# Second-norm vectors spread by TensorE instead of a broadcast load, and a rearranged routing, in a two-layer retention, convolution and MoE step

## Chip, cores and metric

The kernel runs on one core of one Trainium2 chip. The metric is the device time of one execution in microseconds (us). All matrices are float32; where it matters a matrix product is made from a high and a low part in the fp32r format. Engines are named as in the profile: PE is TensorE, DVE VectorE, ACT ScalarE, POOL GpSimd, and SP the queue that issues most DMAs.

## What is computed

256 tokens (128 of a prompt, 128 of a sample, `NT` = 2 tiles) of width 1024 go through two layers. Each layer is a token mixer, a norm, a mixture of experts and a second norm:

```python
for i in range(DEPTH):                     # DEPTH = 2
    sh1, sc1, g1, sh2, sc2, g2 = split(silu(cond) @ ada_w[i] + ada_b[i], 6)
    h = x * (1 + sc1) + sh1
    y = retention(h) if i == 0 else short_conv(h)
    x = layer_norm(ALPHA * x + g1 * y, ln_g[i, 0], ln_b[i, 0])
    h = x * (1 + sc2) + sh2
    y = moe_ffn(h)                         # 64 experts, top 6 of 4 of 8 groups, plus one shared
    x = layer_norm(ALPHA * x + g2 * y, ln_g[i, 1], ln_b[i, 1])
```

In `moe_ffn` the score of a group is the sum of its two best experts, the four best groups are kept, and of the experts in them the six best.

## The kernel before

**Weights.** All weights, some 500 MB, pass once through a ring of 14 slots of 1 MB in SBUF (`Stream`). The loads are written into SP's queue in the order of the program: a unit is issued when the unit 14 places before it has been marked as used. Every other load that SP issues stands in the same queue, in order: `spread` (L537) is such a load, one row of DRAM written to all 128 partitions, 512 KB for a vector of 1024.

**Order.** Within a stage each engine works through its instructions in the order of the program; waits between engines are semaphores. Tiles are taken by tag: a new tile of a tag waits until the readers of the last one of that tag are done. The PSUM banks 0 to 3 are such tags too (`bank`; `rtbank` alternates between banks 2 and 3).

**Stages.** Retention with its adaLN matmuls; the first norm and the router (`ln1`, `router`, `router_turn`); the choice of experts (`route`); 24 blocks of experts (`moe`); the second norm, which also makes the modulated input of the next mixer (`ln2_next`); the convolution (`conv`); then norm, router, choice and blocks of layer 1, and `ln2_out`. Between the last blocks of a layer stands a branch (`overflow`) that all engines reach.

**First norm and routing.** `ln1` makes the input of the MoE, `hf`, for the two tiles. `parts` splits it: ScalarE rounds it to H (L1034), GpSimd subtracts to get the low part L (L1035). `router_turn` makes scores and the best groups (`gr`, in which the entries of the four kept groups are replaced by HIT). `route` turns that into a mask: L1142 to L1147 make a group mask and a penalty and apply them, L1150 takes the maxima, L1154 to L1156 give `maskb`, TensorE counts (L1160 to L1166, into two banks `bk` and `cnt`), L1171 and L1277 (in `slots`) make the 0/1 matrix P0 of slots, and L1176 to L1192 the weights and the order of the experts; L1185 and L1187 read `cnt`. `moe` then gathers the tokens of the first four blocks by matmuls with P0 (`gather`, L1305; four calls on banks 0, 1, 2, 3, each with 8 matmuls on H and L, copied out by L1309), and the first expert matmul (L1343) follows.

**Second norm of layer 0.** The normalised value stands in tile `g2`, tag G. TensorE turns it, and `mod_evac` makes the convolution's input as H and L (L670 to L677). `ln2_gb` has issued two broadcast loads of ln_g and ln_b to tiles of tags T5 and T6; GpSimd multiplies both by ALPHA (L1532) and updates x by

```python
nc.gpsimd.tensor_mul(self.x[:, t], xh, lgb[0])              # L1002, xh is a half of tile G
nc.gpsimd.tensor_add(self.x[:, t], self.x[:, t], lgb[1])    # L1003
```

for each of the two tiles.

**Convolution.** `conv` takes a new tile of tag G and writes the product of two projections to it (L1610, L1613), after which L1618 and L1620 convolve it. Its weights come in pieces of 512 columns: ScalarE rounds a piece to its high half (L139), VectorE subtracts to get the low half (L140), both inputs in SBUF, and TensorE uses a piece in 12 matmuls (L691 to L693). Four pieces make a projection (`proj_T`), four pieces fit in SBUF at a time, and adaLN matmuls (L503) stand between the projections.

**End of layer 1.** `end` issues the two broadcasts of ln_g and ln_b to tag H after the branch and ahead of the last two blocks; `ln2_out` uses them.

Of the kernel before, what the change touches and what calls it, by code (L numbers as in the profile page):

```python
# [7 lines left out]
F32 = mybir.dt.float32  # L8
# [3 lines left out]
AF = mybir.ActivationFunctionType  # L12
OP = mybir.AluOpType
AX = mybir.AxisListType

D = 1024
KD = 8
NT = 2
# [5 lines left out]
ALPHA = (2.0 * 2) ** 0.25  # L24
EPS = 1e-5
SENT = 3.0e38
HIT = 3.2e38
HIT_T = 3.1e38
# [43 lines left out]
class Kernel:  # L72
# [343 lines left out]
    def load_layer_consts(self, l):  # L416
        I, q = self.I, self.nc.sync
        q.dma_start(out=self.rb, in_=I["moe_bias"][l:l + 1].to_broadcast([128, NEXP]))
        for t in range(NT):
            for j, n in ((0, "ln_g"), (64, "ln_b")):  # L420
                q.dma_start(out=self.lnr[j + t:j + 64:32], in_=I[n][l, 0].rearrange("(h c) -> h c", h=2))

    def load_router(self, l):
        self.rw = self.w([128, KD, NEXP], F32, "S3")
# [580 lines left out]
    def ln1(self, ada=False):  # L1005


        nc = self.nc
        hf = []
        g = self.g1  # L1010
        self.ln_open(g, hf)
        mu, rs, _ = self.ln_x
        self.h2T = [self.w([128, 4, NT * 128], F32, f"T{7 + i}") for i in range(2)]

        def scale(t):
            nc.vector.scalar_tensor_tensor(self.A[t], g[:, t], mu[t], self.A[t], op0=OP.add, op1=OP.mult)

        def norm(t):
            v = [x.rearrange("n (p j) -> n p j", j=KD) for x in (self.A[t], self.B[t])]
            for h in range(2):  # L1020
                js = slice(4 * h, 4 * h + 4)
                nc.vector.scalar_tensor_tensor(hf[t].rearrange("n (j p) -> n p j", j=KD)[:, :, js], v[0][:, :, js], rs[t],
                                               v[1][:, :, js], op0=OP.mult, op1=OP.add)

        def turn(t):
            for half in range(2):
                bk = self.pjbank()
                for c in range(4):
                    k = 4 * half + c
                    nc.tensor.transpose(bk[:, 128 * c:128 * (c + 1)], hf[t][:, 128 * k:128 * (k + 1)], self.ident)  # L1030
                nc.scalar.copy(self.h2T[half][:, :, 128 * t:128 * (t + 1)], bk.rearrange("p (c n) -> p c n", c=4))

        def parts(t):
            nc.scalar.copy(H[:, t], hf[t])  # L1034
            nc.gpsimd.tensor_sub(L[:, t], hf[t], H[:, t].bitcast(F32))  # L1035

        hf.append(self.w([128, D], F32, "W", 4))
        for h in range(2):
            self.ln_part(0, h)
        scale(0)  # L1040
        self.table(AF.Sigmoid)
        self.ln_part(1, 0)
        norm(0)
        turn(0)
        hf.append(self.w([128, D], F32, "W", 4))
        self.ln_part(1, 1)
        self.router(0)
        scale(1)
        norm(1)
        self.h2 = [self.w([128, NT, D], F32R, "H"), self.w([128, NT, D], F32R, "L")]  # L1050
        H, L = self.h2
        if ada:
            bk = self.ada_mm(1, 0, range(4, 6), self.free_acc(0), True, False)
        self.warm(self.WN[ada])
        turn(1)
        self.router_turn(0)
        self.router(1)
        self.router_turn(1)
        parts(0)
        parts(1)  # L1060
        self.table(AF.Silu)
        if ada:
            self.ada_mm(1, 0, range(6, 8), bk)
            self.ada_bk = bk
        self.warm(self.WN[2 + ada])
# [68 lines left out]
    def route(self, l):  # L1134
        nc = self.nc
        V = nc.vector
        sc = self.scores
        tmp, gr = self.rtmp, self.gr
        sel = mask = tmp[:, 0:128].rearrange("p (t e) -> p t e", t=NT)
        gmask = self.w([128, NT, 8], F32, "gmask")  # L1140
        pen = self.w([128, NT, 8], F32, "pen")
        V.tensor_scalar(gmask, gr[:, :, 0:8], HIT_T, None, op0=OP.is_ge)  # L1142
        V.tensor_scalar(pen, gmask, 1.0, SENT, op0=OP.subtract, op1=OP.mult)
        sm = self.selm[:, :, 0:64].rearrange("p t (g e) -> p t g e", e=8)
        V.tensor_mul(sm, sel.rearrange("p t (g e) -> p t g e", e=8),
                     gmask[:, :, :, None].to_broadcast([128, NT, 8, 8]))
        V.tensor_add(sm, sm, pen[:, :, :, None].to_broadcast([128, NT, 8, 8]))  # L1147
        m8 = self.w([128, NT, 8], F32, "m8")
        for t in range(NT):
            V.max(out=m8[:, t], in_=self.selm[:, t, 0:64])  # L1150
        V.memset(m8[:, :, 6:8], SENT)
        res = tmp[:, 260:392].rearrange("p (t e) -> p t e", t=NT)
# [5 lines left out]
        bk = self.rtbank()  # L1158
# [6 lines left out]
        for t in range(NT):  # L1165
# [5 lines left out]
        V.scalar_tensor_tensor(self.r1, bk[:, 0:128].rearrange("p (t e) -> p t e", t=2), 1.0, mask,  # L1171
                               op0=OP.add, op1=OP.mult)
        self.P0 = self.slots(0, self.r1)
        ws = self.w([128, NT], F32, "ws")
        for t in range(NT):
            V.scalar_tensor_tensor(self.comb[:, t], sc[:, t], 1.0, mask[:, t], op0=OP.mult, op1=OP.mult,  # L1176
# [116 lines left out]
    def gather(self, P, xg, q, j2, b=2):  # L1293
# [14 lines left out]
                    n += 1  # L1308
        nc.scalar.copy(xg[j2 // 2][:, 2 * (j2 % 2):2 * (j2 % 2) + 2], bk.rearrange("p (c n) -> p c n", c=2))  # L1309

    def slot_T(self, Pc, i):

        nc = self.nc
        o = 128 * (i % 4)
        bk = self.bank(2)
        for t in range(NT):
            nc.tensor.transpose(bk[:, 128 * t:128 * (t + 1)], Pc[:, t, o:o + 128], self.ident)
        PT = self.w([128, NT * 128], F32R, f"S{i % 2}")
        cb = self.w([128, 1], F32, "cb", 2)
        nc.vector.tensor_scalar(PT, bk[:, 0:256], 0.0, None, op0=OP.is_gt)  # L1320
        nc.vector.tensor_reduce(out=cb, in_=bk[:, 0:256], axis=AX.X, op=OP.add)
        return PT, cb

    def moe(self, l, fill, first):
        self.new_acc()
        for n, i in enumerate((self.SH[0],) * 2 + (self.SH[1],) * 2 + (self.SH[2],)):
            fill.setdefault(i, []).append((self.shared, l, n))
        nc, U, st = self.nc, self.U, self.st
        n = self.nb
        P, C, X, G = {}, {}, {}, {}  # L1330
# [57 lines left out]
        nq = n // 2  # L1388
        prep(0)
        C[0] = self.weighted(P[0], 0)  # L1390
        for j in range(4):
            self.gather(P[0], X[0], 0, j, j)
        for f in first:
            f()
        fill.setdefault(0, []).insert(0, (self.order,))
# [54 lines left out]
            pair(i)  # L1450

        def end():
            if l == self.layers - 1:
                t = self.w([128, 2, D], F32, "H")
                self.ln2_gb(l, [t[:, 0], t[:, 1]])
            self.ln_open(self.g2, [self.w([128, D], F32, f"T{7 + t}") for t in range(NT)])
            for i in range(n - self.END, n):
                pair(i)
# [46 lines left out]
        for t in range(NT):  # L1505
            self.spread(self.g2[:, t], self.vecs[1][t, 1:2])

    def ln2_gb(self, l, tiles):

        self.lgb = tiles  # L1510
        for x, n in zip(tiles, ("ln_g", "ln_b")):
            self.spread(x, self.I[n][l, 1:2])

    def ln2_next(self):

        nc = self.nc
        g = self.g2
        mu, rs, nm = self.ln_x
        self.ln2_gb(0, [self.w([128, D], F32, "T5"), self.w([128, D], F32, "T6")])
        banks = [[self.bank(2 * t + h) for h in range(2)] for t in range(NT)]  # L1520
        for t in range(NT):
            nc.vector.tensor_scalar(g[:, t], g[:, t], mu[t], rs[t], op0=OP.add, op1=OP.mult)
        ks = range(self.HEAD1)
        ada = self.ada_mm(1, 1, ks, self.free_acc(0), True)
        for t in range(NT):
            for h in range(2):
                self.mod_T(t, g[:, t], h, banks[t][h])
        self.warm(self.WN[4], self.free_acc(1))
        self.mod_evac(banks, self.a1, self.b1)
        self.ada_sum(1, 1, ks, ada)  # L1530
        for i in range(2):
            nc.gpsimd.tensor_scalar(self.lgb[i], self.lgb[i], ALPHA, 1.0, op0=OP.mult, op1=OP.mult)  # L1532
        for t in range(NT):
            self.next_x(t, g[:, t], self.lgb)

# [193 lines left out]
```

## Time and profile before

| what | value |
|---|---|
| median of 3 runs | 1470.44 us (1468.39 to 1474.17) |
| the profiled execution | 1470.57 us |
| its span, first to last instruction | 1468.8 us |
| TensorE busy | 1305.3 us, 89% of the span |
| VectorE, ScalarE, GpSimd busy | 475.8, 396.7, 101.6 us |
| moved by DMA | 535.32 MB, mean 364 GB/s |
| mean granted clock of TensorE | 0.959 |

The span is what the trace covers; the execution's own time is a little longer. A granted clock of 1.0 is 2.4 GHz, 0.5 is 1.2 GHz. Busy time of TensorE holds matmuls that are pipelined, so a busy TensorE is not one at its peak. A DMA share of 1 means that all 16 DMA engines were busy.

### The profile page before, as it was taken

Reading aid. Unit: us, or ns where it says so; the run is one execution under the profiler, and the core shown is the slowest. Engines: PE = TensorE matmul, PEld = TensorE weight load, DVE = VectorE, ACT = ScalarE, POOL = GpSimd, SP = SyncE. Lnnn points to the kernel's source line nnn. Section 1 sums busy time; section 2 is a strip of 40 time slices with the busy share of each in tenths; the row PEclk is TensorE's granted clock in tenths of the full one; section 3 lists DMA queues with packets and bytes.
Section 4 is the critical chain, followed back from the end, with each engine's and each line's share of the span. In section 5 each row is a group of like instructions: output and inputs, shape, how many; then the busy total and the mean of one; then the engine's idle time right before and its main releaser. Section 6 shows DMA issues by size and latency. Waiting matters only on the chain. (4 is left out here: it accounts for less than half of the span.)

```text
span 1468.8 us, 21018 instructions
## 1 busy us (share of the span) xinstructions
PE 1305.3 (89%) x7542; PEld 711.2 (48%) x7542; DVE 475.8 (32%) x943; ACT 396.7 (27%) x704; POOL 101.6 (7%) x140
## 2 busy tenths in 40 slices
PE   6899999889999889998768699799999889998774
PEld 4788888544435323443214488654445224443211
DVE  4665656732121111211004366822211011121004
ACT  5654545422221012221103234422221012221001
POOL 3120110230000000000001300220000000000001
PEclk9999999999999989999988899999999999999998
DMA  9999796989999999999999998679999999999995
GB/s 286 324 382 349 261 333 244 349 318 375 408 391 415 413 407 413 412 398 409 411 368 393 364 386 301 229 242 394 398 398 411 411 403 413 408 393 409 397 364 197
DMA packets 169343, 535.32 MB, mean 364 GB/s; under 512 B 14212, under 2 KB 65596, under 8 KB 148244
## 3 DMA queue, kind: packets, MB, share of 16 engines
q1 hardware_dynamic: 166148, 529.25, 94.3%
q10 hardware_dynamic: 2768, 4.60, 0.9%
q8 instruction: 62, 1.02, 0.3%
q14 instruction: 45, 0.37, 0.1%
q0 software_dynamic: 320, 0.08, 0.0%
HBM read 528.57 MB, written 5.31 MB: 363 GB/s over the span
## 5 line engine op out<-in xcount | busy, mean ns | idle before, releaser
L1343 PE MATMUL b<-ring,W 128*32 128x512 f32 (+1 forms) x2048 | 440.9, 626 | 63.6 <-DMA ring<-in_moe_w_up 59.2
L1374 DVE SCALAR_TENSOR_TENSOR Y<-b,cb,Y 128x512 fp32r<-128x512 f32 x92 | 69.1, 751 | 675.0 <-ACT Y L1373 675.0
L1343 PEld LDWEIGHTS b<-ring,W 128*32 128x32 f32 (+1 forms) x2048 | 104.4, 124 | 293.4 <-issue 268.1
L1370 PE MATMUL b<-ring,mtmp 128*32 128x512 f32 (+1 forms) x1024 | 221.8, 631 | 17.6 <-DMA ring<-in_moe_w_down 17.3
L1373 ACT ACTIVATE Y<-b,cb 128x512 fp32r<-128x512 f32 x92 | 63.2, 687 | 423.7 <-PE b L1370 393.4
L140 DVE TENSOR_TENSOR W<-ring,W 128x512 fp32r<-128x512 f32 x198 | 135.5, 707 | 91.8 <-ACT W L139 91.4
L139 ACT CAST W<-ring 128x512 fp32r<-128x512 f32 x197 | 117.9, 621 | 105.7 <-PE b L693 78.2
L1370 PEld LDWEIGHTS b<-ring,mtmp 128*32 128x32 f32 (+1 forms) x1024 | 58.4, 130 | 160.6 <-issue 101.9
L691 PE MATMUL b<-H,W 128*128 128x256 f32 x400 | 115.6, 289 | 14.3 <-DVE G L1613 12.1
L693 PE MATMUL b<-H,W 128*128 128x256 f32 x400 | 114.3, 286 | 4.2 <-DVE W L140 4.2
L692 PE MATMUL b<-L,W 128*128 128x256 f32 x400 | 114.1, 285 | 0.1
L1305 PE MATMUL b<-T,H 128*128 128x256 f32 x384 | 99.9, 293 | 6.5 <-ACT W L1309 1.5
L121 PE MATMUL acc<-Y,S 128*128 128x512 f32 x368 | 100.6, 396 | 0.0
L1305 PEld LDWEIGHTS b<-T,H 128*128 128x128 f32 x384 | 72.8, 190 | 52.7 <-PE b L1343 41.0
L1305 PE MATMUL b<-T,L 128*128 128x256 f32 x384 | 95.5, 283 | 0.0
L691 PEld LDWEIGHTS b<-H,W 128*128 128x128 f32 x400 | 77.7, 194 | 24.1 <-issue 13.8
L1309 ACT COPY W<-b 128x512 f32<-128x512 f32 x96 | 56.4, 587 | 105.6 <-PE b L1305 105.6
L693 PEld LDWEIGHTS b<-H,W 128*128 128x128 f32 x400 | 77.6, 194 | 4.7 <-DVE W L140 4.5
L692 PEld LDWEIGHTS b<-L,W 128*128 128x128 f32 x400 | 77.6, 194 | 0.4 <-issue 0.3
L1305 PEld LDWEIGHTS b<-T,L 128*128 128x128 f32 x384 | 73.2, 191 | 0.0
L121 PEld LDWEIGHTS acc<-Y,S 128*128 128x128 f32 x368 | 63.0, 188 | 11.8 <-issue 3.4
L995 POOL TENSOR_SCALAR lnst<-lnst 128x1 f32<-128x1 f32 x8 | 1.8, 230 | 880.9 <-DVE G L988 485.9
(327 smaller groups left out, 1283.8 us busy)
## 6 DMA issues: line engine op xcount, KB each, us to landing
ring<-in_moe_w_gate SPq DMA_DIRECT2D x256, 512.0 KB
ring<-in_moe_w_up SPq DMA_DIRECT2D x256, 512.0 KB
ring<-in_moe_w_down SPq DMA_DIRECT2D x120, 1024.0 KB
ring<-in_ada_w SPq DMA_DIRECT2D x48, 1024.0 KB
ring<-in_ret_w_in SPq DMA_DIRECT2D x20, 1024.0 KB
ring<-in_conv_w_in SPq DMA_DIRECT2D x12, 1024.0 KB
ring<-in_ret_w_out SPq DMA_DIRECT2D x8, 1024.0 KB
ring<-in_moe_w_down SPq DMA_DIRECT2D x16, 512.0 KB
```

What stands on the lines that cost most here:

```text
L121: self.nc.tensor.matmul(self.acc[t][h], lhsT, rhs, start=s, stop=stop, skip_group_check=True)
L139: (copy or nc.scalar.copy)(hi, src)
L140: nc.vector.tensor_sub(lo, src, hi.bitcast(F32))
L691: nc.tensor.matmul(o, hi[:, c], H[:, k], start=(k == 0), stop=False)
L692: nc.tensor.matmul(o, hi[:, c], L[:, k], start=False, stop=False)
L693: nc.tensor.matmul(o, lo[:, c], H[:, k], start=False, stop=(k == KD - 1))
L1305: nc.tensor.matmul(o, part[:, t, 128 * j:128 * (j + 1)], P[:, t, s0:s0 + 256], start=(n == 0), stop=(n == 3))
L1309: nc.scalar.copy(xg[j2 // 2][:, 2 * (j2 % 2):2 * (j2 % 2) + 2], bk.rearrange("p (c n) -> p c n", c=2))
L1343: nc.tensor.matmul(G[0][m * e:m * (e + 1)], xg[k // 4][:, k % 4, o + m * e:o + m * (e + 1)], w[:, :, k % 4], start=(k == 0), stop=(k == KD ...
L1370: nc.tensor.matmul(bk[m * e:m * (e + 1)], hT[:, k, m * e:m * (e + 1)], w[:, k, 512 * h:512 * (h + 1)], start=(k == 0), stop=(k == 1))
L1373: nc.scalar.activation(hi, bk, AF.Copy, scale=cb)
L1374: nc.vector.scalar_tensor_tensor(lo, bk, cb, hi.bitcast(F32), op0=OP.mult, op1=OP.subtract)
```

## The change

- `load_layer_consts` loads a third row beside the two that it loads twice: ln_g and ln_b of the second norm go to partitions 2, 34, 66 and 98 of the tile `lnr` (two small loads more per layer).
- `ln2_gb` no longer loads. After block 11 of each layer TensorE multiplies a column of the identity, repeated 128 times, with `lnr`, which puts one half of ln_g or ln_b on all partitions; ScalarE copies it to a tile of tag G1 and multiplies by ALPHA on the way in layer 0. The four broadcast loads (two in `ln2_next`, two in `end`) and GpSimd's two multiplications L1532 are gone.
- The low parts L of the MoE input are made by VectorE, in `route` behind P0 and ahead of the weights and the order of the experts.
- The four instructions of the group mask are replaced by one per tile, the minimum of `gr` - HIT_T and the score.
- The first gather goes over H of both tiles, then L of both tiles, and writes all four banks in each of these four rounds; the copies follow at the end.

```diff
     def load_layer_consts(self, l):
-        for t in range(NT):
+        for i, t in ((0, 0), (0, 1), (1, 2)):
             for j, n in ((0, "ln_g"), (64, "ln_b")):
-                q.dma_start(out=self.lnr[j + t:j + 64:32], in_=I[n][l, 0].rearrange("(h c) -> h c", h=2))
+                q.dma_start(out=self.lnr[j + t:j + 64:32], in_=I[n][l, i].rearrange("(h c) -> h c", h=2))
...
-        def parts(t):
-            nc.scalar.copy(H[:, t], hf[t])
-            nc.gpsimd.tensor_sub(L[:, t], hf[t], H[:, t].bitcast(F32))
...
-        parts(0)
-        parts(1)
+        for t in range(NT):
+            nc.scalar.copy(H[:, t], hf[t])
+        self.hf = hf
...
-        gmask = self.w([128, NT, 8], F32, "gmask")
-        pen = self.w([128, NT, 8], F32, "pen")
-        V.tensor_scalar(gmask, gr[:, :, 0:8], HIT_T, None, op0=OP.is_ge)
-        V.tensor_scalar(pen, gmask, 1.0, SENT, op0=OP.subtract, op1=OP.mult)
-        sm = self.selm[:, :, 0:64].rearrange("p t (g e) -> p t g e", e=8)
-        V.tensor_mul(sm, sel.rearrange("p t (g e) -> p t g e", e=8),
-                     gmask[:, :, :, None].to_broadcast([128, NT, 8, 8]))
-        V.tensor_add(sm, sm, pen[:, :, :, None].to_broadcast([128, NT, 8, 8]))
         m8 = self.w([128, NT, 8], F32, "m8")
         for t in range(NT):
+
+            V.scalar_tensor_tensor(self.selm[:, t, 0:64].rearrange("p (g e) -> p g e", e=8),
+                                   gr[:, t, 0:8, None].to_broadcast([128, 8, 8]), HIT_T,
+                                   sel[:, t].rearrange("p (g e) -> p g e", e=8), op0=OP.subtract, op1=OP.min)
             V.max(out=m8[:, t], in_=self.selm[:, t, 0:64])
...
         self.P0 = self.slots(0, self.r1)
+        for t in range(NT):
+            H, L = self.h2
+            V.tensor_sub(L[:, t], self.hf[t], H[:, t].bitcast(F32))
         ws = self.w([128, NT], F32, "ws")
...
+    def gather_first(self, P, xg):
+
+        nc = self.nc
+        bks = [self.bank(j) for j in range(4)]
+        for n, (t, part) in enumerate((t, p) for p in self.h2 for t in range(NT)):
+            for j in range(KD):
+                nc.tensor.matmul(bks[j // 2][:, 256 * (j % 2):256 * (j % 2 + 1)], part[:, t, 128 * j:128 * (j + 1)],
+                                 P[:, t, 0:256], start=(n == j % 2 == 0), stop=(n == 3), skip_group_check=True)
+        for j, bk in enumerate(bks):
+            nc.scalar.copy(xg[j // 2][:, 2 * (j % 2):2 * (j % 2) + 2], bk.rearrange("p (c n) -> p c n", c=2))
...
+        fill.setdefault(self.SH[2] + 1, []).append((self.ln2_gb, ALPHA if l + 1 < self.layers else 1.0))
...
-        for j in range(4):
-            self.gather(P[0], X[0], 0, j, j)
+        self.gather_first(P[0], X[0])
...
-            if l == self.layers - 1:
-                t = self.w([128, 2, D], F32, "H")
-                self.ln2_gb(l, [t[:, 0], t[:, 1]])
...
-    def ln2_gb(self, l, tiles):
-
-        self.lgb = tiles
-        for x, n in zip(tiles, ("ln_g", "ln_b")):
-            self.spread(x, self.I[n][l, 1:2])
+    def ln2_gb(self, scale):
+
+        g = self.w([128, 2, D], F32, "G1")
+        self.lgb = [g[:, 0], g[:, 1]]
+        for j in range(4):
+            bk = self.bank(2 + j % 2)
+            r = 32 * j + 2
+            self.nc.tensor.matmul(bk, self.ident[:, r:r + 1].to_broadcast([128, 128]), self.lnr, start=True, stop=True)
+            self.nc.scalar.activation(g[:, j // 2, 512 * (j % 2):512 * (j % 2 + 1)], bk, AF.Copy, scale=scale)
...
-        self.ln2_gb(0, [self.w([128, D], F32, "T5"), self.w([128, D], F32, "T6")])
...
-        for i in range(2):
-            nc.gpsimd.tensor_scalar(self.lgb[i], self.lgb[i], ALPHA, 1.0, op0=OP.mult, op1=OP.mult)
```

## Rows read from the trace of the kernel before

**Rows 1.** Page: busy tenths of the DMA engines in 40 slices.
```profile
DMA  9999796989999999999999998679999999999995
```

**Rows 2.** Windows: busy us (instructions) of each engine, granted clock, DMA share, GB/s.
```profile
core 0: us, PE busy (x) PEld busy (x) DVE busy (x) ACT busy (x) POOL busy (x), PEclk, DMA share, GB/s
829.20:841.20 12.00, 0.00 (x1) 0.03 (x1) 0.82 (x3) 0.00 (x0) 9.99 (x6) 0.67 1.02 369
...
846.60:850.20 3.60, 3.60 (x18) 3.60 (x18) 2.91 (x8) 0.87 (x2) 0.00 (x0) 0.50 0.99 396
821.60:825.20 3.60, 3.60 (x32) 3.60 (x31) 0.73 (x2) 1.24 (x2) 0.00 (x0) 1.00 1.05 392
```

**Rows 3.** TensorE's waits, 840 to 940 us: total us, times, longest us.
```profile
PE b L691 <- DVE G L1613: 12.1, 1, 12.1
PE b L693 <- DVE W L140: 4.2, 1, 4.2
```

**Rows 4.** Timeline, second norm of layer 0: start, us, instruction, [idle before <- releaser].
```profile
803.80 2.52 POOL L677 TENSOR_TENSOR L<-T,H 128x1024 fp32r<-128x1024 f32 x1 [3.32 <-ACT H L676]
...
804.70 2.71 DVE L677 TENSOR_TENSOR L<-T,H 128x1024 fp32r<-128x1024 f32 x1 [0.60 <-ACT H L676]
...
807.08 1.22 POOL L489 DMA_DIRECT2D adaS<-in_ada_b  x2 [0.29 <-POOL adaS L486]
...
820.28 1.07 PE L503 MATMUL b<-ring,cs 128*32 128x512 f32 x8
...
825.04 0.33 SPq L537 DMA_DIRECT2D T<-in_ln_g  x1
...
829.66 1.04 POOL L1532 TENSOR_SCALAR T<-T 128x1024 f32<-128x1024 f32 x1 [21.36 <-DMA T<-in_ln_g]
...
840.23 0.43 DVE L1610 TENSOR_TENSOR G<-b,mtmp 128x256 f32<-128x256 f32 x1 [17.89 <-POOL x L1002]
```

**Rows 5.** Timeline, routing of layer 0.
```profile
289.50 4.66 POOL L1035 TENSOR_TENSOR L<-W,H 128x1024 fp32r<-128x1024 f32 x2 [5.99 <-ACT H L1034]
...
290.26 1.62 DVE L1142 TENSOR_SCALAR gmask<-gr 128x16 f32<-128x16 f32 x1
...
291.92 2.27 DVE L1143 TENSOR_SCALAR pen<-gmask 128x16 f32<-128x16 f32 x1
...
294.75 0.35 DVE L1150 MAX8 m<-mtmp 128x8 f32<-128x64 f32 x2
...
297.20 1.43 DVE L1277 TENSOR_TENSOR T<-rc,cp 128x256 fp32r<-128x256 f32 x4
...
299.88 0.20 DVE L1187 TENSOR_SCALAR od<-b,tie 64x1 f32<-64x1 f32 x1
...
304.20 5.37 PE L1343 MATMUL b<-ring,W 128*64 128x512 f32 x24
```

**Rows 6.** Timeline, routing of layer 1.
```profile
951.50 0.35 DVE L1150 MAX8 m<-mtmp 128x8 f32<-128x64 f32 x2
...
960.49 5.37 PE L1343 MATMUL b<-ring,W 128*64 128x512 f32 x24
```

**Rows 7.** Windows in and after the routing of layer 0.
```profile
291.60:296.50 4.90, 0.02 (x2) 0.01 (x1) 4.24 (x13) 0.27 (x2) 2.56 (x2) 0.75 1.05 422
...
306.00:309.00 3.00, 3.00 (x18) 0.98 (x14) 0.00 (x0) 1.17 (x2) 2.74 (x2) 1.00 0.09 15
```

**Rows 8.** Timeline, VectorE's subtractions in the first stage.
```profile
106.22 3.35 DVE L140 TENSOR_TENSOR W<-ring,W 128x512 fp32r<-128x512 f32 x4
...
160.69 1.22 DVE L794 TENSOR_TENSOR Y<-G,Y 128x1024 fp32r<-128x1024 f32 x1 [1.11 <-ACT Y L793]
```

**Rows 9.** Timeline, SP's queue, end of the blocks of layer 1.
```profile
1404.66 0.34 SPq L537 DMA_DIRECT2D H<-in_ln_g  x1
...
1407.24 0.34 SPq L228 DMA_DIRECT2D ring<-in_moe_w_gate  x1
```

**Rows 10.** Window in a block of four experts of layer 0.
```profile
485.00:500.00 15.00, 10.47 (x44) 2.10 (x42) 0.75 (x1) 0.69 (x1) 0.00 (x0) 0.77 1.03 410
```

## The prediction, made blind

> **What bounds the kernel now.** I read the slices of the page first. The DMA engines are at 90% or more in 33 of 40 slices [rows 1], so time can be won only where they stand still or where bytes go away. The slices that fall short belong to the first stage, to the stretch from the second norm of layer 0 to the routing of layer 1, and to the end. In the blocks of the MoE the ring hides small delays; at the stage boundaries it does not, because TensorE waits there for something that is not a ring slot.
>
> Second, the windows around the second norm of layer 0 and TensorE's waits. From 829.2 to 841.2 us TensorE starts one matmul, and afterwards it runs at half the clock (18 matmuls in 3.6 us where the undisturbed stretch has 32) [rows 2]. Its two waits are 12.1 us for VectorE's L1613 and 4.2 us for L140 [rows 3]. Third, the timeline says who is late: VectorE's L1610, the first instruction of the convolution to write tile G, sat idle for 17.9 us until GpSimd's L1002 had read G, and GpSimd sat idle for 21.4 us until ln_g had landed. SP issued that broadcast only at 825.0 us, behind ring loads [rows 4]. So a load of 512 KB in the wrong place of a queue stops TensorE.
>
> Fourth, the timeline of the routing. L1142 and L1143 work on 16 elements and take 1.62 and 2.27 us; they end when the two GpSimd subtractions L1035 end (289.50 + 4.66 = 294.16 us) [rows 5]. The two engines exclude each other there.
>
> **The change, part by part.**
>
> *Boundary between the layers.* The broadcasts and GpSimd's multiplication by ALPHA go, so x is updated as soon as GpSimd is free: after its DMA issue, at 808.3 us [rows 4]. The wait on tile G goes with it. Its cost now is 12.1 + 4.2 us [rows 3] and the slow clock after it, 20 matmuls at 0.20 in place of 0.11 us, 1.8 us [rows 2]: 18.1 us. Late next is the port. The four x updates, 2.33 us each by the price of L1035 [rows 5], now lie beside the splits of the convolution's first weights, where VectorE makes the low halves (L140). That such a pair excludes each other is seen at L677: VectorE's half takes 2.71 us and ends 1.1 us after GpSimd's half [rows 4], and the same kind of subtraction takes 1.22 us alone [rows 8]. Queued behind a blocked L140 are all later low halves and then L1610. I take it that the two engines alternate: updates at 808.3, 811.3, 814.3 and 817.3 us, one L140 between them (0.7 us: half the elements of L794, [rows 8]), so the low halves of pieces 3 to 6 are ready at 811.3, 814.3, 817.3 and 820.3 us. TensorE uses a piece in about 1.4 us (12 matmuls), so the second projection ends three pieces after 820.3, at 824.6 us. Now it ends at 820.3, where the next adaLN matmuls start [rows 4]. The loss is 4.3 us, and the gain 18.1 - 4.3 = 13.8 us. Bounds: 18.1 if the port costs nothing; if GpSimd runs its four updates without letting VectorE in, 9.4 us go, and some 2 us more for a fallen clock, which leaves 6.7 us. The ring can follow a gain of this size, since slices 25 to 27 show the DMA engines at 0.8, 0.6 and 0.7 [rows 1].
>
> The nearest row of a split beside GpSimd is weaker: four L140 take 3.35 us beside L881 [rows 8], some 0.6 over four times 0.7, but L881 has one input from SBUF and ends in their middle. The Trainium skill (SBUF — State Buffer, "Who interferes with whom") says that a VectorE instruction with two SBUF inputs is fully blocked by a GpSimd instruction that reads SBUF. It speaks against this part of the change. By the weak row the boundary would gain about 17 us and the kernel would come to 1450 us; by the rule it is the 13.8 us above.
>
> *Routing.* Four VectorE instructions go; two come, one before each maximum, at about 0.22 us each like the maxima (0.35 for two) [rows 5]. From 290.26 to the end of the maxima it takes 0.8 us instead of 4.84. In layer 1 the maxima end at 951.85 [rows 6] and the pattern is the same, so there they end near 947.1. But the low parts now stand in VectorE's queue after L1277, two of 1.22 us [rows 8], and behind them are all instructions up to L1187. L1185 and L1187 read the counts from a PSUM bank that route took from banks 2 and 3. The new gather writes all four banks in its first eight matmuls. So TensorE stops after four or six of them until L1187 is done. Now L1187 ends (300.08 us) 1.45 us after L1277 (298.63) and nobody waits for it [rows 5]; with the low parts in between it is 1.45 + 2.4 = 3.85 us. L1277 ends 3.53 us after the maxima [rows 5], hence at 294.6, and the bank is free at 298.45. TensorE has then been idle for some 3.3 us. In the idle stretch of 4.9 us before L1160 the mean granted clock was 0.75 [rows 7], so it fell to half about 2.5 us into it; I expect it to fall again. The 20 to 22 matmuls to the end of bank 0 at 0.20 us are 4.2, and the result, its copy and handovers 0.95 us: block 0 starts at 303.6 where it now starts at 304.2 [rows 5]. Gain 0.6 us. Layer 1 by the same count: 947.1 + 3.5 + 3.85 + 5.15 = 959.6 against 960.49 [rows 6], 0.9 us. There ln1_scale on GpSimd is no longer behind L1035 and may meet the scaling before the router (one multiplication of 1.04 us, as L1532 in rows 4), half of which I take off: 0.4. Bounds for both layers: 0; with the clock kept (0.11 us per matmul) 2.5 and 2.3; without the wait for the bank 5.7 and 5.4 us. What is won there passes on, as the DMA engines moved 15 GB/s from 306 to 309 us [rows 7]: they waited for block 0.
>
> *End.* Two broadcasts of 512 KB leave SP's queue in layer 1. Now they are issued from 1404.66, and the ring goes on at 1407.24 [rows 9]: 2.6 us earlier, in a stretch in which the DMA engines are full to the last load [rows 1]. Gain 2.6 us; between 0 (TensorE late instead) and 3.5.
>
> *Block 11.* TensorE gets four plain-f32 matmuls of 512 columns, ScalarE four copies. Two such matmuls side by side, 64 columns of the array each, take 24 in 5.37 us [rows 5], 0.45 us per matmul and so 0.9 per pair; four over the full array are 3.6 us. Cover: a block of four experts, in which TensorE is busy for 10.5 of 15 us [rows 10]. I take 0. Without the cover 3.6, or 6.8 if every copy (0.7) and handover lies between two matmuls, in each layer.
>
> *Row loads.* Two more small ones per layer in SP's queue, about 0.5 us of issue each. The ring's slots cover them: 0, at most 1 us per layer.
>
> Sum: 13.8 + 0.6 + 0.4 + 2.6 = 17.4 us. The profiled execution took 1470.57 (its span is 1468.8, the rest lies around it), the median of the runs is 1470.44; 1470.6 - 17.4 = 1453.2, so 1453 us.
>
> **The rivals.**
>
> *The routing gives what it looks like giving.* If the clock holds through the wait, both layers give 4.8 together, the sum is 21.2, and the time is 1449. If the gather does not wait for the bank, 11.1, the sum is 27.5, and the time 1443. For it: the low parts alone would be in time, the second is ready before the last eight matmuls. Against it: the order of instructions in VectorE's queue, and the clock in rows 7.
>
> *The port costs more.* GpSimd keeps it for all four updates: boundary 6.7, sum 10.3, time 1460. For it: L1035's two ran in 4.66 us without a gap although VectorE wanted in [rows 5]. Against it: L1142 did get in between them.
>
> *The DMA engines are the bound everywhere.* Then only bytes count: four broadcasts, 2.1 MB, at some 0.4 MB/us [rows 2] 5 us, time 1465. Against it: the 12 us in which TensorE waited for a tile and the 3 us in which DMA stood still.
>
> *Slower.* Block 11: TensorE has no idle left in the blocks that follow, and its additions push everything. It decides alone from 8.7 us per layer on (half the sum). The rows give 3.6, at most 6.8, and idle time beside it. With 9 us it would be 1471 or more.
>
> **How the numbers follow.** Forecast 0.56 (its own range 1448 to 1457); routing gives more 0.19; port costs more 0.17; DMA everywhere 0.05; slower 0.03. A change of 0.5%, 7.4 us, is about what a measurement of this kernel can tell. The first three are all faster by more: 0.92; the fourth is "same", 0.05; the last slower, 0.03. The range 1444 to 1461 holds the first three almost wholly.
>
> **What would show it.** No idle of VectorE before L1610 and no TensorE gap after 829 us; L140s of 2 to 3 us beside the x updates; maxima within a microsecond of the last match; TensorE stopped in the gather until the counts have been read, with the clock at half after it; SP's first ring load after the branch at the time of the broadcast now. Wrong would make it: no stop in the gather (time below 1449), a TensorE gap over 5 us at the head of the convolution (above 1457), or a wait for the first norm's vectors at the end of the convolution, should the ring not follow.

## The result, and the profile after

| kernel | median, us | runs | ratio to the kernel before, 95% interval |
|---|---|---|---|
| before | 1472.31 (1468.39 to 1477.49) | 4 | |
| changed | 1454.1 (1448.27 to 1454.56) | 4 | 0.9872 [0.9852, 0.9892] |
| changed, second set | 1451.12 (1447.84 to 1454.25) | 5 | 0.987 [0.9844, 0.9896] |
| changed, third set | 1453.73 (1450.69 to 1456.66) | 5 | 0.9886 [0.9864, 0.9907] |

The kernel before, run beside the second and the third set, took 1470.05 us (17 runs) and 1468.96 us (11 runs). The change makes the kernel 15 to 19 us faster, some 1.2%. The forecast was 1453. The profiled executions of the first two sets (1448.27 and 1447.84 us) are the fastest of theirs, so the stretches below are given for the profiled executions of all three sets.

**The head of the convolution.** The windows of [rows 2] first, now in the changed kernel:

```profile
829.20:841.20 12.00, 12.00 (x101) 8.86 (x100) 7.53 (x14) 4.22 (x8) 0.00 (x0) 1.00 1.03 392
846.60:850.20 3.60, 3.60 (x35) 2.76 (x27) 2.95 (x8) 0.62 (x1) 0.00 (x0) 1.00 1.02 364
```

The same times lie later in the work now. Where TensorE started one matmul in 12 us it starts 101, and the granted clock is 1.00 in both windows (0.50 in the second before). The timeline of the second norm shows what took the place of the stall:

```profile
806.14 1.23 POOL L489 DMA_DIRECT2D adaS<-in_ada_b  x2 [0.29 <-POOL adaS L486]
806.39 0.68 DVE L140 TENSOR_TENSOR W<-ring,W 128x512 fp32r<-128x512 f32 x1
...
807.39 2.41 POOL L1002 TENSOR_TENSOR x<-G,G 128x1024 f32<-128x1024 f32 x1
807.65 12.31 DVE L140 TENSOR_TENSOR W<-ring,W 128x512 fp32r<-128x512 f32 x6
809.88 2.73 POOL L1003 TENSOR_TENSOR x<-x,G 128x1024 f32<-128x1024 f32 x1
812.57 2.84 POOL L1002 TENSOR_TENSOR x<-G,G 128x1024 f32<-128x1024 f32 x1
815.49 2.72 POOL L1003 TENSOR_TENSOR x<-x,G 128x1024 f32<-128x1024 f32 x1
...
823.09 1.07 PE L503 MATMUL b<-ring,cs 128*32 128x512 f32 x8
...
825.05 0.41 DVE L1615 TENSOR_TENSOR G<-b,mtmp 128x256 f32<-128x256 f32 x1
```

GpSimd updates x as soon as its two DMAs are issued, and L1615 (L1610 of before, [rows 4]) follows without idle. The price is seen on L140: 0.68 us alone at 806.39, but six of them take 12.31 us, the first four beside the four updates. Two of TensorE's waits over the whole execution (total us, times, longest us) are that price and that of the routing:

```profile
PE b L1313 <- DVE od L1183: 5.8, 2, 3.0
...
PE b L693 <- DVE W L140: 2.8, 3, 1.1
```

The waits of 12.1 and 4.2 us [rows 3] have become three of at most 1.1. L1313 is the new first gather.

**The routing of layer 0.** The timeline, to be held against [rows 5]:

```profile
288.04 0.21 DVE L1140 SCALAR_TENSOR_TENSOR mtmp<-gr,mtmp 128x64 f32<-128x64 f32 x1
...
288.68 0.23 DVE L1143 MAX8 m<-mtmp 128x8 f32<-128x64 f32 x1
...
291.92 1.04 PE L1313 MATMUL b<-T,H 128*128 128x256 f32 x6
292.13 2.35 DVE L1169 TENSOR_TENSOR L<-W,H 128x1024 fp32r<-128x1024 f32 x2
...
295.74 0.20 DVE L1183 TENSOR_SCALAR od<-b,tie 64x1 f32<-64x1 f32 x1
...
296.00 2.50 PE L1313 MATMUL b<-T,H 128*128 128x256 f32 x10 [3.04 <-DVE od L1183]
...
298.30 3.62 PE L1313 MATMUL b<-T,L 128*128 128x256 f32 x16
```

The mask and both maxima take 0.8 us, from 4.9. What follows gives most of it back: six matmuls of the gather, then a stop of 3.04 us until L1183 has read the counts, behind the two low parts (L1169). The matmuls after the stop run at half the clock (granted clock 0.50 from 296.0 to 301.8 us; x16 in 3.62 us).

**The end of the convolution.** VectorE's first multiplication for the first norm of layer 1 (L1016) did not wait before (first line), and now waits for its vectors (second):

```profile
930.89 1.28 DVE L1016 SCALAR_TENSOR_TENSOR T<-G,lnst,T 128x1024 f32<-128x1024 f32 x1
...
916.21 1.28 DVE L1016 SCALAR_TENSOR_TENSOR T<-G,lnst,T 128x1024 f32<-128x1024 f32 x1 [1.32 <-DMA T<-vecA]
```

**Where the time went**, as the lengths of stretches between single instructions in the profiled executions (differences of starts or ends in their timelines; the stretches of one execution add up to its span). The group match is the MATCH_REPLACE8 that writes `gr`; its end counts:

| stretch, us | before | changed, three executions | gain, mean |
|---|---|---|---|
| start to the last group match of layer 0 | 290.2 | 288.1, 288.2, 289.3 | 1.7 |
| to block 0's first matmul (L1343, now L1351) | 14.0 | 13.7, 12.5, 12.7 | 1.0 |
| to the second norm (L1522, now L1529) | 493.4 | 494.8, 493.8, 497.1 | -1.8 |
| to the second product of the convolution (L1627, now L1632) | 50.8 | 36.0, 35.5, 36.0 | 15.0 |
| to the first L1016 | 82.4 | 83.6, 84.5, 83.3 | -1.4 |
| to the last group match of layer 1 | 15.4 | 15.9, 16.8, 15.5 | -0.7 |
| to block 0 of layer 1 | 14.2 | 13.0, 11.0, 13.0 | 1.9 |
| to the end | 508.3 | 501.4, 503.7, 505.7 | 4.7 |
| span | 1468.8 | 1446.5, 1446.1, 1452.5 | 20.4 |

Between executions of one kernel the last stretch differs by up to 4 us, the third by 3, block 0 of layer 1 by 2, and the others by 0.5 to 1.3. The kernel before has one execution here. Two kernels of the experiments that keep its boundary take 51.6 and 53.0 us from the second norm to the second product, so the gain there is 15 to 17 us.

### The profile page after: what moved, and what is told of

Read it like the earlier page. It is cut to its first block, busy times and chain, and to the rows that moved or that the text cites. A ratio compares the mean times of both kernels' runs of the same rounds, so it can differ in the third digit from the quotient of the medians.

```text
span 1446.5 us, 21047 instructions
## 1 busy us (share of the span) xinstructions
PE 1311.2 (91%) x7558; PEld 713.0 (49%) x7558; DVE 481.4 (33%) x943; ACT 400.5 (28%) x712; POOL 92.5 (6%) x134
## 3 DMA queue, kind: packets, MB, share of 16 engines
q8 instruction: 62, 1.02, 0.3%
## 4 chain that ended last, share of the span: by engine, by line
DMA 45%; PE 42%; DVE 6%; SPq 3%; issue 2%; ACT 1%; POOL 1%; ACTq 0%; DVEq 0%; POOLq 0%
DMA ring<-in_moe_w_up 26%; DMA ring<-in_moe_w_down 14%; PE b L1351 11%; PE b L1378 6%; PE acc L121 5%; PE b L691 3%; PE b L693 3%; PE b L1301 3%; PE b L692 3%; DMA ring<-in_moe_w_gate 3%; SPq L197 2%; PE b L503 1%; DVE W L140 1%; DMA ring<-in_ada_w 1%; PE b L709 1%
## 5 line engine op out<-in xcount | busy, mean ns | idle before, releaser
L1351 PE MATMUL b<-ring,W 128*32 128x512 f32 (+1 forms) x2048 | 437.7, 628 | 57.5 <-DMA ring<-in_moe_w_up 52.7
L1382 DVE SCALAR_TENSOR_TENSOR Y<-b,cb,Y 128x512 fp32r<-128x512 f32 x92 | 69.1, 751 | 671.0 <-ACT Y L1381 671.0
L1351 PEld LDWEIGHTS b<-ring,W 128*32 128x32 f32 (+1 forms) x2048 | 104.6, 125 | 284.3 <-issue 260.9
L140 DVE TENSOR_TENSOR W<-ring,W 128x512 fp32r<-128x512 f32 x198 | 143.9, 750 | 84.6 <-ACT W L139 84.1
L1301 PE MATMUL b<-T,H 128*128 128x256 f32 x352 | 91.5, 293 | 6.3 <-ACT W L1305 1.4
L1301 PEld LDWEIGHTS b<-T,H 128*128 128x128 f32 x352 | 66.3, 188 | 52.2 <-PE b L1351 41.1
L1301 PE MATMUL b<-T,L 128*128 128x256 f32 x352 | 87.5, 282 | 0.0
L1305 ACT COPY W<-b 128x512 f32<-128x512 f32 x88 | 51.6, 586 | 84.1 <-PE b L1301 84.1
L1301 PEld LDWEIGHTS b<-T,L 128*128 128x128 f32 x352 | 66.7, 189 | 0.0
L1368 ACT COPY mtmp<-b 128x256 f32<-128x256 f32 x48 | 17.9, 372 | 156.5 <-PE b L1366 156.5
```

The lines of the kernel that those rows point to most:

```text
L140: nc.vector.tensor_sub(lo, src, hi.bitcast(F32))
L1301: nc.tensor.matmul(o, part[:, t, 128 * j:128 * (j + 1)], P[:, t, s0:s0 + 256], start=(n == 0), stop=(n == 3))
L1351: nc.tensor.matmul(G[0][m * e:m * (e + 1)], xg[k // 4][:, k % 4, o + m * e:o + m * (e + 1)], w[:, :, k % 4], start=(k == 0), stop=(k == KD ...
L1382: nc.vector.scalar_tensor_tensor(lo, bk, cb, hi.bitcast(F32), op0=OP.mult, op1=OP.subtract)
```

## The experiments

**The change again**, twice, without an edit:

> The changed kernel once more, beside the three that follow on the same chip, as their yardstick. Both theories: 18 to 19 us faster than before (ratio 0.987 to 0.988).

> The changed kernel itself, on the same chip, as the base of the two beside it: a ratio of 0.987 to the kernel before, as in its first two runs.

Measured: the second and third lines of the first table.

**Only the vectors by TensorE.** The kernel before with this part of the change alone (row loads, matmuls and copies, no broadcasts, no multiplication on GpSimd):

```diff
-        for t in range(NT):
+        for i, t in ((0, 0), (0, 1), (1, 2)):
...
+        fill.setdefault(self.SH[2] + 1, []).append((self.ln2_gb, ALPHA if l + 1 < self.layers else 1.0))
...
-        self.ln2_gb(0, [self.w([128, D], F32, "T5"), self.w([128, D], F32, "T6")])
...
-        for i in range(2):
-            nc.gpsimd.tensor_scalar(self.lgb[i], self.lgb[i], ALPHA, 1.0, op0=OP.mult, op1=OP.mult)
```

> Before with only the second norm's vectors put on the partitions by TensorE after block 11; routing and low parts as before. My theory (the broadcast load behind ring loads stops the convolution's first writes, 13.8 us; two broadcasts in SP's queue at the end, 2.6 us): 16.4 us faster than before, range 13 to 19; no wait of TensorE for L1613 of 12 us, L1610 no longer idle 17.9 us. Rival (the routing carries the gain): under 6 us faster.

Measured: 1453.4 us, ratio 0.9882 [0.9857, 0.9907], 17 us faster. From the second norm to the second product it takes 35.3 us, as in the whole change.

**Only the routing.** The kernel before with the other part (mask in one step, low parts by VectorE behind P0, the new first gather):

```diff
-            nc.gpsimd.tensor_sub(L[:, t], hf[t], H[:, t].bitcast(F32))
...
+        for t in range(NT):
+            H, L = self.h2
+            V.tensor_sub(L[:, t], self.hf[t], H[:, t].bitcast(F32))
...
-        for j in range(4):
-            self.gather(P[0], X[0], 0, j, j)
+        self.gather_first(P[0], X[0])
```

> Before with only the routing part (mask in one step, low parts by VectorE, first gather by H then L); the second norm's vectors loaded as before. My theory (the wait for the counts' bank takes the gain back): 1 us faster, range 0 to 3, in each layer a stop of about 3 us between the sixth and seventh matmul of the first gather. Rival (the maxima come 4 us sooner in each layer and pass it on): 8 to 11 us faster.

Measured: 1467.33 us over 12 runs, ratio 0.9984 [0.9969, 1.0]: some 2.7 us, and the interval reaches to no change. Here the boundary is as slow as before (51.6 us), so the two parts are told apart: most of the gain is the vectors'. The two parts alone, 17 and 2.7 us, add up to the whole change beside them (18.9 us) within the noise.

**Only the mask in one step**, with the low parts still on GpSimd:

```diff
-        V.tensor_scalar(gmask, gr[:, :, 0:8], HIT_T, None, op0=OP.is_ge)
...
+            V.scalar_tensor_tensor(self.selm[:, t, 0:64].rearrange("p (g e) -> p g e", e=8),
+                                   gr[:, t, 0:8, None].to_broadcast([128, 8, 8]), HIT_T,
+                                   sel[:, t].rearrange("p (g e) -> p g e", e=8), op0=OP.subtract, op1=OP.min)
```

> Before with only the mask in one step; low parts by GpSimd and the gather as before. My theory (the port, not the number of instructions, makes the mask slow): the minimum has two inputs from SBUF and is held by GpSimd's subtractions, so the maxima end 3.5 to 4.5 us after the last match as before (4.84), and time is 0 to 1 us from before. Rival (four instructions against two): the maxima end 0.8 us after the match, and block 0 starts 4 us sooner.

Measured in one run: 1468.21 us, no difference that one run can tell. The timeline says why the count of instructions was not the cost:

```profile
287.29 4.65 POOL L1035 TENSOR_TENSOR L<-W,H 128x1024 fp32r<-128x1024 f32 x2 [6.00 <-ACT H L1034]
...
287.95 1.79 DVE L1143 SCALAR_TENSOR_TENSOR mtmp<-gr,mtmp 128x64 f32<-128x64 f32 x1
...
289.91 2.12 DVE L1143 SCALAR_TENSOR_TENSOR mtmp<-gr,mtmp 128x64 f32<-128x64 f32 x1
```

The same instruction that takes 0.21 us in the changed kernel takes 1.79 and 2.12 us while L1035 runs, and each ends within 0.1 us of the end of one of the two subtractions. The maxima end 4.27 us after the match (4.9 before, 0.8 in the changed kernel). A kernel with the four old instructions and no subtraction on GpSimd was not run, so what the one step is worth by itself is not shown.

**The counts read before the low parts.** The changed kernel with the two instructions that read the counts' bank, and the tile that they write, moved ahead of the low parts:

```diff
         self.P0 = self.slots(0, self.r1)
+        self.od = od = self.w([128, 6, NEXP], F32, "od")
...
+        V.tensor_copy(self.cnt, cnt[:, 0:64])
+        V.tensor_scalar(kc, cnt[0:64, 64:65], 64.0, self.tie[0:64, NEXP:NEXP + 1], op0=OP.mult, op1=OP.add)
         for t in range(NT):
             H, L = self.h2
             V.tensor_sub(L[:, t], self.hf[t], H[:, t].bitcast(F32))
```

> The changed kernel with the two instructions that read the counts moved ahead of the low parts, nothing else. My theory: the first gather runs through without a stop and at the full clock, block 0 starts 4 to 5 us sooner in each layer, and the kernel is 8 to 10 us faster than the changed one (ratio to before about 0.981). Rival (the low parts themselves hold the gather, or the ring can't follow): less than 2 us faster than the changed kernel.

Measured: 1440.96 us (1439.52 to 1446.39), ratio 0.9808 [0.9781, 0.9836]. On the same chip as the second set of the change it is 10.2 us faster than that. The timeline of layer 0:

```profile
292.19 2.24 PE L1313 MATMUL b<-T,H 128*128 128x256 f32 x16
292.40 0.22 DVE L1170 COPY od<-b 128x64 f32<-128x64 f32 x1
292.53 0.20 DVE L1171 TENSOR_SCALAR od<-b,tie 64x1 f32<-64x1 f32 x1
292.66 2.34 DVE L1174 TENSOR_TENSOR L<-W,H 128x1024 fp32r<-128x1024 f32 x2
294.14 1.99 PEld L1313 LDWEIGHTS b<-T,L 128*128 128x128 f32 x16
294.26 2.08 PE L1313 MATMUL b<-T,L 128*128 128x256 f32 x16
...
296.30 4.15 PE L1351 MATMUL b<-ring,W 128*64 128x512 f32 x18
```

and the window over the gather:

```profile
291.00:296.30 5.30, 5.30 (x44) 5.11 (x45) 5.16 (x18) 0.64 (x2) 0.00 (x0) 1.00 1.04 418
```

The gather runs through at a clock of 1.00. From the match to block 0 it takes 7.9 us in layer 0 and 8.0 in layer 1, where the change takes 13.0 and 12.4 (means of three) and the kernel before 14.0 and 14.2. That is 9.4 us over both layers, nearly the whole difference of 10.2: the time won in the routing passes on.

**The port's price at the boundary** (the port is the prediction's word for that by which VectorE and GpSimd exclude each other). The changed kernel without the update of x after the second norm of layer 0 (it leaves out GpSimd's four operations, so layer 1 goes on with another x):

```diff
-        for t in range(NT):
-            self.next_x(t, g[:, t], self.lgb)
```

> The changed kernel without the update of x by the second norm of layer 0 (four GpSimd instructions left out; x keeps the value of the first norm, so layer 1 computes with another residual). My theory (the port is held by these four): the L140s at the head of the convolution all take about 0.7 us, TensorE does not wait for them, and the second adaLN step of the convolution starts 4.3 us sooner; of this 0 to 4 us reach the end, as VectorE already waits 1.3 us for the first norm's vectors at the end of the convolution. Rival (the long L140s have another cause): they stay at 2 to 3 us.

Measured: 1449.43 us, ratio 0.9851 [0.9818, 0.9883]. The boundary takes 32.3 us in place of 35.8, and L140 is back at its own price:

```profile
808.71 1.89 DVE L140 TENSOR_TENSOR W<-ring,W 128x512 fp32r<-128x512 f32 x3
```

So the port costs 3.5 us there. The next stretch gives most of it back: from the second product to the first L1016 it takes 86.9 us in place of 83.8, and VectorE waits there 3.2 us for a vector at L987 and 1.7 us at L1016. What SP's queue brings did not come sooner.

**The additions of the update later in the program.** The counts first, and the two additions of x taken out of the update and put at the end of the second of the four passes of `conv`'s loop:

```diff
-            self.next_x(t, g[:, t], self.lgb)
+            nc.gpsimd.tensor_mul(self.x[:, t], g[:, t], self.lgb[0])
...
+            if m == 1:
+                for t in range(NT):
+                    nc.gpsimd.tensor_add(self.x[:, t], self.x[:, t], self.lgb[1])
```

> The kernel with the counts read first, and in addition the two additions of the x update moved from the second norm to the second group of the convolution, where pieces lie ready ahead. My theory: half of the 4.3 us at the head of the convolution comes back, and 0 to 2 us of it reach the end, as the vectors of the first norm are late next. Rival (the port hardly costs): no difference to the kernel with the counts read first. If the additions stop TensorE in their new place: slower than it.

Measured: 1443.04 us over 6 runs, ratio 0.9816 [0.9792, 0.9841]: no gain over the counts first. GpSimd waits for nothing there, so the additions began at 808.62, straight behind the multiplications. The boundary even took 38.5 us; the windows show the clock down in it (1.00 in the changed kernel from 807 to 823 us), and why it fell is open:

```profile
804.00:814.00 10.00, 6.92 (x44) 6.42 (x43) 10.00 (x4) 1.86 (x3) 9.94 (x8) 0.80 1.04 390
814.00:820.00 6.00, 6.00 (x39) 4.11 (x39) 3.65 (x6) 2.10 (x4) 0.00 (x1) 0.76 1.05 385
```

**The broadcasts put back**, all four (two tensors at two places), with nothing that reads them; twice, and each place by itself:

```diff
+        for x, n in zip(tiles, ("ln_g", "ln_b")):
+            self.spread(x, self.I[n][l, 1:2])
```

> The changed kernel with all four broadcast loads put back where they stood in SP's queue, into the old tiles, read by nobody. My theory (what counted at the second norm was the wait, not the bytes): 2.6 us slower than the changed kernel, all of it at the end, where SP's first ring load after the branch comes 2.6 us later; nothing in the convolution. Rival (bytes count wherever the DMA engines are full): 5 us slower than the changed kernel. If the load itself had been the whole cost: 16 us slower.

> The changed kernel with only the two broadcasts at the second norm of layer 0 put back; nothing reads what they bring. Both broadcasts of 1 MB together, here and at the end, cost 7 us over the change in e4 where 2.6 were expected. Theory, place: about two thirds of that lie here. The loads stand in the queue ahead of the refill of a ring that TensorE has just drained, so the refill, the first norm's vectors of layer 1 and its first expert weights come 2 to 3 us later, and that is not made up: 4 to 5 us over the change, with VectorE waiting longer for the vectors at the end of the convolution. Rival, bytes alone: 1 MB at 0.41 MB/us, 2.6 us. Rival, hidden: the DMA engines have idle slices here, 0 to 1 us.

> The changed kernel with only the two broadcasts at the end of the blocks of layer 1 put back; nothing reads what they bring. Theory: 2.6 us over the change, the time by which the ring's loads are moved back in the queue, at the end of a stretch in which the DMA engines are full. Rival: TensorE or the eviction is late there, 0 to 1 us. If e4's 7 us lie here, 5 us or more.

> The changed kernel with both pairs of broadcasts put back, unread, once more. Alone, each pair cost 1.5 to 2 us over the change on the same chip, while both together had cost some 9 us in another set. Theory, spread of the executions: the stretches between the events vary by 2 to 5 us from one profiled execution to the next, and the 9 us were partly that; a ratio of 0.990 to 0.991 to the kernel before, 2 to 4 us over the change. Rival, the two pairs add up to more than their sum: 0.993 again, 7 us or more over the change.

| kernel | median, us | ratio, 95% interval | faster than before on the same chip, us |
|---|---|---|---|
| all four back | 1458.25 | 0.9931 [0.9909, 0.9953] | 10.7 |
| all four back, again | 1456.3 | 0.9905 [0.9889, 0.9921] | 13.3 |
| only at the boundary | 1454.18 | 0.9898 [0.9875, 0.9921] | 14.8 |
| only at the end | 1455.3 | 0.9896 [0.9874, 0.9918] | 13.7 |
| the change, beside the two above | 1453.73 | 0.9886 [0.9864, 0.9907] | 15.2 |

The first of these missed its expectation: the change is 17.4 us faster than before in the mean of its three sets, so 6.7 us were gone where 2.6 or 5 were expected. The repeat lost 4.1. Each place alone lost 0.5 and 1.6 us to the change beside it, where 4 to 5 and 2.6 were expected, and the intervals can't tell that from nothing. So part of the first figure was the spread of the executions, and the rival of the last expectation (7 us or more once again) is not borne out. What the four loads cost lies between some 2 and 7 us; bytes alone would be 5, and this isn't settled.

For the loads at the boundary the waits of VectorE show the place (total us, times, longest):

```profile
DVE G L987 <- DMA G<-vecG: 3.0, 1, 3.0
DVE T L1016 <- DMA T<-vecA: 1.6, 1, 1.6
```

The second product to the first L1016 takes 86.6 us, 2.8 more than in the change. It does so in all three kernels with these loads (86.5 to 86.7 us; 82.3 to 84.8 in the profiled executions of the change and of four kernels that update x without these loads), so the expectation that nothing would change in the convolution missed too. In the execution with the loads only at the boundary both routings and the last stretch were 1 to 2 us shorter than the change's mean, so its total shows nothing of it. With the loads only at the end, they hold the ring up by what was forecast: the broadcasts go out from 1390.38 and the next ring load at 1392.97, 2.6 us later.

## Why the prediction was right

**Boundary, 13.8 us: right in the mechanism, 1 to 3 us low.** The three executions gained 15.0 us in the mean over the one execution of before. The stall [rows 3, 4] went as a whole, and the four updates did collide with L140. The two engines took turns, one L140 to one update; the first two of the six, each in a narrower window of VectorE's timeline:

```profile
807.65 2.71 DVE L140 TENSOR_TENSOR W<-ring,W 128x512 fp32r<-128x512 f32 x1
...
810.28 2.88 DVE L140 TENSOR_TENSOR W<-ring,W 128x512 fp32r<-128x512 f32 x1
```

Four take 2.71 to 2.88 us each beside the four updates, the last two follow alone. The fourth, for the sixth piece, ends 11.4 us after the first update starts, where I had 12.0 (808.3 to 820.3). The price, 4.3 us forecast, is 3.5 by the kernel without the updates, and the gain without it is 18.5 us by the same kernel, where I had 18.1. The rival in which GpSimd keeps the port for all four updates (6.7 us) is refuted by the same rows. The cheap reading from [rows 8], by which the port would cost almost nothing, falls too. The Trainium skill (SBUF — State Buffer, "Who interferes with whom"), by which a VectorE instruction with two SBUF inputs contends with a GpSimd instruction that reads SBUF, and the contention is an exclusive lock, agrees with this trace: 0.68 us alone, 2.71 and more beside an update.

**What the boundary gave back: foreseen as a way to be wrong, and not put into the sum.** The two stretches behind it are 2.1 us longer together: the first norm's vectors are late by 1.0 to 1.8 us at L1016. I had named this wait and left it at nothing, because slices 25 to 27 of [rows 1] show the DMA engines at 0.8, 0.6 and 0.7. That reading failed for the stretch that counts. In the changed kernel (first line) the DMA engines are full from 860 to 904 us (1.02 to 1.05), and the vectors are issued from 908.83 us. In the kernel before (second line) they had time to spare shortly ahead of the vectors, issued from 918.18 us:

```profile
890.00:900.00 10.00, 10.00 (x85) 10.00 (x85) 4.90 (x8) 4.74 (x9) 0.00 (x0) 1.00 1.02 410
...
914.00:918.00 4.00, 4.00 (x35) 4.00 (x35) 2.47 (x7) 1.86 (x3) 0.00 (x0) 1.00 0.36 133
```

SP's queue in the change, from 860 to 925 us, waits for:

```profile
SPq L531 <- DMA ring<-in_moe_w_down: 4.0, 2, 2.1
SPq L537 <- DMA vecG<-adaS: 4.0, 1, 4.0
```

L531 writes the vectors to DRAM and L537 reads them back. Before, L531 did not wait for ring loads, and L537 waited 1.9 us. By these rows the ring did not follow the whole gain, and the vectors in its queue came late.

**Routing, 0.6 and 0.4 us: right in the mechanism; 1.0 and 1.9 measured from the match to block 0.** The stop in the gather came after six matmuls (four or six forecast), it lasted 3.04 us (3.3), and the bank was free 7.8 us after the match (8.2). The term that varied is the clock. The gather after the stop in layer 0 of the first set stands above (2.50 and 3.62 us). In the second set, layer 0 and layer 1:

```profile
296.06 2.50 PE L1313 MATMUL b<-T,H 128*128 128x256 f32 x10 [3.03 <-DVE od L1183]
298.37 2.41 PE L1313 MATMUL b<-T,L 128*128 128x256 f32 x16
...
939.00 1.46 PE L1313 MATMUL b<-T,H 128*128 128x256 f32 x10 [2.78 <-DVE od L1183]
940.30 2.08 PE L1313 MATMUL b<-T,L 128*128 128x256 f32 x16
```

The clock fell to half in five of the six cases of the change, as I had taken it, but not at one moment: in the first set it was 0.50 as soon as the gather went on, in the third still 0.80 and 0.93 over the next ten matmuls and 0.55 and 0.53 over the last sixteen. In layer 1 of the second set it stayed at 1.00 (939.0 to 942.3 us). My price for the case that it stays, 2.5 and 2.3 us gained, is passed by that case (3.2). The scaling before the router in layer 1, for which I took off half of 1.04 us, did meet VectorE:

```profile
930.41 1.05 POOL L1091 TENSOR_SCALAR Y<-Y 128x1024 f32<-128x1024 f32 x1 [5.58 <-DMA Y<-in_ln_g]
...
930.78 0.69 DVE L1126 TENSOR_TENSOR gse<-mtmp 128x8 f32<-128x8 f32 x1
...
931.99 0.78 DVE L1140 SCALAR_TENSOR_TENSOR mtmp<-gr,mtmp 128x64 f32<-128x64 f32 x1
```

The two take 0.17 and 0.21 us in layer 0, so this costs 1.1 us here and 0.7 in the other two executions; part of it lies ahead of the match. The rival without a wait for the bank (5.7 and 5.4 us) is not what the change does, but its price was right: with the counts read first the two layers gain 6.1 and 6.2 us over the kernel before.

**End, 2.6 us: consistent, not shown by itself.** From block 0 of layer 1 to the end the six profiled executions with the two loads take 506.6 us in the mean (504.5 to 508.4), the eight without them 503.7 (501.4 to 505.8), 2.9 us less. The kernel with only these loads put back is 1.6 us slower than the change beside it, within its interval.

**Block 11, 0: held.** The four matmuls (each stands as two in the trace) take 3.7 us in layer 0 (3.6 forecast), the copies 0.6 each:

```profile
538.26 3.70 PE L1519 MATMUL b<-lnr,cp 128*128 128x512 f32 x8
539.33 0.60 ACT L1520 ACTIVATE G<-b 128x512 f32<-128x512 f32 x1 [1.22 <-PE b L1519]
```

The block behind them makes up for it. VectorE's next two evictions (L1374, now L1382) start 243.7 and 251.9 us after block 0's first matmul before, and 246.9 and 250.7, 245.8 and 249.7, 249.8 and 253.7 us in the three executions of the change: the first is 2 to 6 us later, the second between 2 us sooner and 2 us later. The rival by which this stretch makes the kernel slower falls, and so does the one by which only bytes count: the vectors alone gained 17 us, where the bytes would be 5.

**Row loads, 0: not seen in the time, but in the queue.** I had 0.5 us of issue each. At the boundary the two new ones stand much longer in SP's queue:

```profile
821.57 0.47 SPq L421 DMA_DIRECT2D lnr<-in_ln_g  x1
824.48 0.47 SPq L421 DMA_DIRECT2D lnr<-in_ln_b  x1
827.06 0.34 SPq L425 DMA_DIRECT2D S<-in_moe_router  x1
827.49 0.38 SPq L184 DMA_DIRECT2D ring<-in_ada_w  x1
```

The profile puts waits of 2.4 and 2.0 us there down to earlier ring loads, and the DMA engines fall to 0.46 from 825 to 830 us:

```profile
825.00:830.00 5.00, 5.00 (x43) 4.88 (x41) 4.68 (x13) 1.86 (x3) 0.00 (x0) 1.00 0.46 135
```

The ring goes on 30.0 to 31.1 us after the start of the second norm in the three executions of the change, and 30.3 to 31.5 us in the three kernels with the old boundary. So without the broadcasts it goes on hardly sooner here. What the row loads alone cost, no run shows.

Sum: 17.4 us forecast from the profiled execution of before. The medians differ by 18.2, 18.9 and 15.2 us. The parts that came out higher (boundary by 1 to 3 us, routing by 1.9) and the vectors' wait, which was left out (2.1), largely cancel. That the forecast lies within 1 us of the first median is in part luck.

## What to carry to other kernels

When an operation moves down an engine's queue, list what stands behind it, and what those instructions hold: here two reads of a PSUM bank of 0.2 us each, behind two subtractions, cost 9 us in a kernel of 1450, and moving them ahead of the subtractions gave that back. Here a stall behind a late load went with the load; look next at the load that is then late in the same queue. And a few microseconds seen in one profiled execution, or one set of runs, are not yet a cause: the four loads put back cost 6.7 us the first time and 4.1 the second.

## What was not expected of the hardware

The same stop does not always cost the clock: after 2.8 to 3.0 us without a matmul, TensorE's 16 matmuls of the second half took 3.62, 2.41 and 3.31 us in layer 0 and 2.55, 2.08 and 3.47 us in layer 1, in three executions of the same program. At a granted clock of 1.00 (2.4 GHz) they take 2.08. From the match to block 0, both layers together, the three executions take 26.8, 23.5 and 25.7 us. The order of instructions is the same in all three; what decides it is open.

GpSimd and VectorE, both with a queue of work on SBUF, handed the port over after each instruction in all three executions of the change: exactly one L140, of 0.68 us alone, ran to each update, and the updates took 2.4 to 2.8 us where the pair at L1035 took 2.33 each [rows 5]. Small instructions are held as well: L1143 of the mask experiment, 64 elements wide, took 1.79 and 2.12 us in place of 0.21.
